# A hybrid trunk layer in fp32 on one core: the second head's query splits are placed behind the first head's maximum, head 0's rows get a queue of their own, and the interleaving table changes

## The chip, the cores and the metric

One core of a Trainium2 chip. The metric is device time in microseconds, from the start to the end of the program on that core. The kernel before was timed in 3 runs: median 1436.8 us, lowest 1436.42, highest 1437.74. A further execution was recorded by the hardware profiler; all profile numbers come from it.

The engines are TensorE (PE, with its weight loads as a row of their own, PEld), VectorE (DVE), ScalarE (ACT), GpSimd (POOL) and SyncE (SP). DMAs can be issued from SP, ACT and POOL. Each engine works through its instructions in order.

## The reference

One layer of a streaming encoder for two groups of rows that share the weights: 1024 frames of a new stream and 32 next frames of a running stream (so 1056 rows, width 1024). Three groups of heads read one input projection; their outputs are joined and go through an output projection; then comes an MLP with squared ReLU, with a layer norm after each half.

```python
proj = x @ prm['w_in']
q_lat, kv_lat, k_rope_raw, u, p_rwkv = jnp.split(proj, IN_SPLITS, axis=-1)
mla_out = mla_mixer(q_lat, kv_lat, k_rope_raw, ...)     # attention, 6 heads
s5_out = s5_mixer(u, ...)                               # S5 diagonal SSM, 16 groups
rwkv_out = rwkv_mixer(p_rwkv, ...)                      # RWKV-7 scan, 6 heads of 64
merged = jnp.concatenate([mla_out, s5_out, rwkv_out], -1)
x = layer_norm(ALPHA * x + merged @ prm['w_out'], ...)
x = layer_norm(ALPHA * x + jnp.square(jax.nn.relu(x @ prm['w_up'])) @ prm['w_down'], ...)
```

The attention's queries are what the change touches: `rms_norm(q_lat) @ w_qb` gives each head 64 columns without rotation ("nope") and 32 that are rotated ("rope"). The rotation is `x*cos + concat(-x2, x1)*sin` over the two halves of the 32. The new stream's queries see keys in chunks of 64 (chunk-causal); the running stream's queries see 512 cached keys and their own 32. Everything is float32.

## The kernel before

**Arithmetic.** A float32 matrix product is made of three reduced-precision ones: each operand x is split into hi (a copy by ACT, L49) and lo = x - hi (a subtraction by DVE, L50), and `mm3` issues hi*hi (L63), lo*hi (L65) and hi*lo (L67) into one PSUM tile. So every operand costs one ACT and one DVE instruction per piece before PE can use it.

**Stages.** Input projection; then `stage_q`, which makes the queries; then `middle`, where attention, the scan and S5 share the engines; then the output projection and the MLP, which take more than half of the time and in which PE is nearly always busy.

**`stage_q`** computes the queries of all six heads as products of 128 rows (two heads' nope columns; or the rope columns of heads 0 to 3 in one tile `qrope`, those of heads 4 and 5 in one of 96 rows, `qropeb`), rotates the rope tiles on DVE (`turn`), and writes the rows of each head into a DRAM buffer `q_d`: 64 nope rows and two pieces of 16 rope rows. In the kernel before, SP issues the writes of heads 0 and 1 (nope) and of the rope pieces of heads 0 to 3; POOL issues the others. In this stretch DVE also ends the inversion of the scan's triangular matrices; its result goes through DRAM (`zt_d` L782, `xt_d` L783) and comes back in another layout as `zb` and `zc` (L794, L795), from which PE builds further pieces with 32x32 products (L805).

**Attention in `middle`.** `attn_setup` issues on SP the loads of the rotated keys (`kr`), head 0's query rows (`q0`, 96 rows), the cached latents (`ct`) and cached rope keys (`kt`), and the extra rows 96 to 127 of the split queries. `attn_first` makes the keys of head 0 (`sck`, L1144), splits keys and queries, and computes, per block of 128 queries, the scores (L63/65/67 into `sc`) whose row maximum (`mx`, L1304) DVE takes. When all nine blocks are done, DVE joins the two halves (`m`, L1309), PE transposes the result (`scm`, L1311), ACT and DVE split it (`mh`, `ml`), and four small DMAs put it into row 96 of the split queries, so that the later score products have the maximum already subtracted. The cached latents and keys are transposed by PE (`sct`) and copied by ACT to `cpast` and `kpast` (L1118); the keys of the cached part need both. `attn_q` loads the next head's rows into the same buffer (tag "q", one buffer, so the load waits until the last head's split has read it) and splits them.

**Order.** Four generators yield after each small step: F (scores and maxima, head by head), O (probabilities, products with the values), S (scan), X (S5). A string of letters, `PLAN`, says whose step comes next; the order of PE's instructions is pinned by it (`issue_after` makes the scheduler place an instruction behind a given one). The other engines' instructions are placed by a list scheduler that respects data, buffers and these marks; the scan's steps have a higher priority. So changing a letter moves PE's work and, through the scheduler, the work of DVE, ACT and the queues.

Of the kernel before, what the change touches and what calls it, by code (L numbers as in the profile page):

```python
# [17 lines left out]
P = 128  # L18
T = 1056
# [26 lines left out]
def split3(g, ps, hi, lo, lo_eng=None):  # L46

    nc = g.nc
    nc.scalar.activation(out=hi, in_=ps, func=AF.Copy)  # L49
    (lo_eng or nc.vector).tensor_tensor(out=lo, in0=ps, in1=hi.bitcast(F32), op=ALU.subtract)  # L50
# [679 lines left out]
def hsl(i):  # L730
    return slice(64 * i, 64 * i + 64)
# [352 lines left out]
def attn_setup(g):  # L1084

    nc = g.nc
    g.wkv = g.ap0.tile([P, 2, 384], F32, tag="wkv", name="wkv")
    nc.sync.dma_start(out=g.wkv, in_=g.a["w_kvb"])
    g.kh, g.kl, g.q2 = [], [], []
    g.kr = g.ap.tile([P, 13 * 3 * 64], F32, tag="vo", name="kr", bufs=1)[:, :T]  # L1090
    nc.sync.dma_start(out=g.kr[64:128], in_=g.kr_d[0:64])
    g.q0 = g.ap.tile([P, T], F32, tag="q", name="q", bufs=1)
    nc.sync.dma_start(out=g.q0[0:96], in_=g.q_d[0])
    g.cpast = g.ap0.tile([P, 512], F32, tag="cpast", name="cpast")
    g.ct = g.ap.tile([P, 4, P], F32, tag="rec", name="ct", bufs=1)
# [38 lines left out]
def attn_first(g):  # L1134

    nc = g.nc
    attn_setup(g)
    qh, ql = g.qs[0] = g.q2[0]  # L1140

    def key(pool, tag, src):
        ps = pool.tile([P, 512], F32, tag=tag, name="sck")
        nc.tensor.matmul(out=ps[:, :src.shape[-1]], lhsT=g.wkv[:, 0, 0:P], rhs=src, start=True, stop=True)  # L1144
        return ps

    def smooth(ps, i, o, n):
        split3(g, ps[hsl(i), :n], g.kh[i][0:64, o:o + n], g.kl[i][0:64, o:o + n])

    def turned(x, c, o, n):  # L1150
        split3(g, x[64:128, c:c + n], g.kh[0][64:128, o:o + n], g.kl[0][64:128, o:o + n])

    def query(s, n):
        split3(g, g.q0[0:96, s:s + n], qh[0:96, s:s + n], ql[0:96, s:s + n])

    mx = attn_max(g, 0, qh, ql)
# [12 lines left out]
    query(512, 544)
    for _ in range(2):  # L1170
        next(mx)
        yield
    c = key(g.pav, "av", g.cpast)
    for _ in range(2):
        next(mx)
        yield
    d = key(g.psc, "sc", g.ckv[:, TP:T])
    turned(g.kpast, 0, TP, 512)
    turned(g.kr, TP, 1536, TS)
    for i in range(2):  # L1180
# [12 lines left out]

def attn_values(g, p):
# [16 lines left out]
def stage_q(g):  # L1211


    nc = g.nc
    i = 0

    def f(name):
        return g.p1.tile([P, T], F32, tag="f", name=name, bufs=5)

    def product(out, w):  # L1220
        nonlocal i
        for s, n in BLK:
            pool, tag = ((g.pfs, "fs"), (g.pt, "pt"))[i % 2]
            i += 1
            ps = pool.tile([P, 512], F32, tag=tag, name="scq")[:, :n]
            for k in range(2):
                nc.tensor.matmul(out=ps[:out.shape[0]], lhsT=w[:, k], rhs=g.qn[:, k, s:s + n], start=k == 0, stop=k == 1)
            nc.scalar.activation(out=out[:, s:s + n], in_=ps[:out.shape[0]], func=AF.Copy)

    wa = f("wqa")[:, :768].rearrange("p (k h c) -> p k h c", k=2, c=64)  # L1230
    wr = f("wqr")[:, :512].rearrange("p (k j x) -> p k j x", k=2, x=P)
    for k in range(2):
        nc.sync.dma_start(out=wa[:, k], in_=g.a["w_qb"][:, k, :, 0:64])
        for h, n, c, j, x in ((0, 4, 64, 0, 0), (0, 4, 80, 0, 64), (4, 2, 64, 1, 0), (4, 2, 64, 1, 32), (4, 2, 80, 1, 64)):
            nc.scalar.dma_start(out=wr[:, k, j, x:x + 16 * n].rearrange("p (h c) -> p h c", c=16), in_=g.a["w_qb"][:, k, h:h + n, c:c + 16])
    qs_ = g.xp.tile([P, KD, T], F32, tag="xl", name="qnope")

    def nope(p):
        q = qs_[:, KD - 3 + p]
        product(q, wa[:, :, 2 * p:2 * p + 2].rearrange("p k h c -> p k (h c)"))  # L1240
        for h in range(2):
            (nc.gpsimd if p else nc.sync).dma_start(out=g.q_d[2 * p + h, 0:64], in_=q[hsl(h)])

    cs, sn = f("ropec"), f("ropes")
    for h in range(4):
        nc.sync.dma_start(out=cs[32 * h:32 * h + 32], in_=g.a["rope"][0:32])
        for a in range(2):
            nc.sync.dma_start(out=sn[64 * a + 16 * h:64 * a + 16 * h + 16], in_=g.a["rope"][48 - 16 * a:64 - 16 * a])

    def turn(name, m, w, heads):  # L1250

        q, t = (g.p1.tile([P, 1152], F32, tag="kk", name=x, bufs=3)[:, :T] for x in (name, name + "t"))
        product(q[0:m], w)
        r = m - 64
        for a in range(2):
            nc.vector.tensor_tensor(out=t[64 * a:64 * a + r], in0=q[64 - 64 * a:64 - 64 * a + r], in1=sn[64 - 64 * a:64 - 64 * a + r], op=ALU.mult)
        nc.vector.tensor_tensor(out=q[0:m], in0=q[0:m], in1=cs[0:m], op=ALU.mult)
        for x in ((slice(0, P),) if r == 64 else (slice(0, r), slice(64, m))):
            nc.vector.tensor_tensor(out=q[x], in0=q[x], in1=t[x], op=ALU.add)
        yield  # L1260
        for j, h in enumerate(heads):
            for a in range(2):
                (nc.sync if h < 4 else nc.gpsimd).dma_start(out=g.q_d[h, 64 + 16 * a:80 + 16 * a], in_=q[64 * a + 16 * j:64 * a + 16 * j + 16])

    ta, tb = turn("qrope", P, wr[:, :, 0], range(4)), turn("qropeb", 96, wr[:, :, 1, 0:96], (4, 5))
    next(ta)
    nope(0)
    next(ta, None)
    next(tb)
    nope(1)  # L1270
    nope(2)
    next(tb, None)


def attn_q(g, h):

    nc = g.nc
    qh, ql = g.q2[h % 2]
    q = g.ap.tile([P, T], F32, tag="q", name="q", bufs=1)
    nc.sync.dma_start(out=q[0:96], in_=g.q_d[h])  # L1280
    if h > 1:
        for x in (qh, ql):
            nc.sync.dma_start(out=x[96:97].bitcast(F32), in_=g.kr_d[33:34])
    for s, n in ((0, 512), (512, 544)):
        split3(g, q[0:96, s:s + n], qh[0:96, s:s + n], ql[0:96, s:s + n])
        yield
    return qh, ql

# [110 lines left out]
def middle(g, scan):  # L1399
# [36 lines left out]


PLAN = (
    "FFFFFFFFSSSSSFFFFFFFFFFFFFFOFFOOSOSSOOOOFOSOSOSOSFSOFOFOOOOOOOOSSXOFSFSOXOFOFOOOOOOSFSFOSSOSXSOFXFSF"
    "OFOSOFXFSFOOSOSFSSOOXOSFSFOSFSOOFOXOOXOFFOSSOFSOOFXOFOOOSOOXOOOSFFOOXOOOSFOSSSFXSSFFOSFOSFFSSFXFFFSF"  # L1440
    "SFOXOFOSOSFXOOSFOOSOSSXOOFOSSOOXOSOFXOOOOOOOFSFOSSOFSSSOXOXOSOOOOFOOFFSFFOXFFFSSFFSSOOXSOSSFFSOXSFOS"
    "OOXOOSOOOFSOOOOOFSOFOOOOFSXOXOFXOXSOSOFXFOSSOOSOSFOSSFXOOOOSSFOXFSFFFSFFFSFFSFFFFSXFSFFOSSXOSOOFSOXO"
    "FOSFSOOOFXOSOOOFSOXFOSSXOSFOOOSOOOOOFXOOSSSSFOOOFFXSOXFOOSOSFSSOOFSFSFFOOSOOOOOOSOOOOSOOOOSOFOOSSOOO"
    "SOOSSOOSOOSOOOOOOOOO"
)


# [1032 lines left out]
```

## Time and profile before

| | |
|---|---|
| median of 3 runs | 1436.8 us (1436.42 to 1437.74) |
| profiled execution, whole | 1437.9 us |
| its span (first to last instruction) | 1436.1 us |
| mean granted PE clock | 0.972 of full |
| busy: PE / PEld / DVE / ACT / POOL | 96% / 86% / 69% / 45% / 8% |
| matrix products | 11520 |
| DMA | 199.48 MB in 149814 packets, mean 139 GB/s |

How to read the rows that follow: a timeline row gives start and length in us, engine, line of the kernel, operation, output and inputs by the program's names, shape, a count, and in brackets how long the engine had been idle before and what released it. A window row gives the busy time of each engine in a stretch, the clock that PE was granted, and the share of the 16 DMA engines in use. A PE that is busy at half clock counts as busy.

### The profile page before, as it was taken

The page shows a single profiled execution, that of the slowest core. Times are in us where ns is not written, and L with a number is a line of the kernel's source. Part 1 is how long each engine was busy: PE and PEld are TensorE (multiplying, and loading weights), DVE is VectorE, ACT ScalarE, POOL GpSimd, SP SyncE. Part 2 cuts the span into 40 slices and gives each one's busy share as a digit, 9 for nine tenths or more (in the row PEclk, how much of TensorE's full clock was granted, in tenths as well). Part 3 has the DMA queues.
Part 4 walks back from the last instruction along what each step waited for, and adds up shares of the span by engine and source line. Part 5 has one row for each costly group of instructions (what it writes and reads, how often), then busy time and mean ns, then how long its engine had stood idle before and what let it go on. Part 6 is the DMA issues. An engine that isn't in the chain of part 4 may idle for free.

```text
span 1436.1 us, 28225 instructions
## 1 busy us (share of the span) xinstructions
PE 1379.4 (96%) x11520; PEld 1241.1 (86%) x11520; DVE 984.5 (69%) x1793; ACT 641.8 (45%) x1129; POOL 112.4 (8%) x228
## 2 busy tenths in 40 slices
PE   9999999699999989999999999999999999999996
PEld 9989898576777767767788999999999999999996
DVE  7676969755566746565869966666655786665577
ACT  6646543324435554552336444443445443434332
POOL 1201300400000000110300000000000000000022
PEclk9999999789799999999999999999999999999998
DMA  5434554852332321244434543444339695354232
GB/s 205 149 125 143 172 158 98 207 124 55 92 101 75 86 80 35 75 133 137 121 107 150 182 154 142 142 143 162 132 118 390 222 322 166 96 176 135 64 103 77
DMA packets 149814, 199.48 MB, mean 139 GB/s; under 512 B 54424, under 2 KB 97100, under 8 KB 149176
## 3 DMA queue, kind: packets, MB, share of 16 engines
q1 hardware_dynamic: 128540, 177.72, 38.8%
q10 hardware_dynamic: 20424, 17.80, 4.1%
q0 software_dynamic: 720, 2.16, 0.5%
q8 instruction: 90, 1.47, 0.4%
q14 instruction: 40, 0.33, 0.1%
HBM read 130.03 MB, written 67.55 MB: 138 GB/s over the span
## 4 chain that ended last, share of the span: by engine, by line
PE 82%; DVE 8%; DMA 4%; ACT 2%; issue 2%; SPq 1%; ACTq 0%; DVEq 0%; POOL 0%; POOLq 0%
PE acc L63 20%; PE acc L67 20%; PE acc L65 20%; PE av L1333 3%; PE sc L63 1%; DMA wo<-in_w_out 1%; PE st L63 1%; PE st L65 1%; PE st L67 1%; PE prt L857 1%; DVE mx L1304 1%; PE sc L67 1%; PE sc L65 1%; PE pti L805 1%; DMA q<-q_d 1%
## 5 line engine op out<-in xcount | busy, mean ns | idle before, releaser
L67 PE MATMUL acc<-xo,wo 128*128 128x256 f32 (+1 forms) x896 | 253.7, 284 | 2.8 <-DVE wo L50 2.6
L63 PE MATMUL acc<-xo,wo 128*128 128x272 f32 (+1 forms) x896 | 254.1, 284 | 0.1
L65 PE MATMUL acc<-xo,wo 128*128 128x272 f32 (+1 forms) x896 | 253.3, 283 | 0.1
L67 PE MATMUL acc<-hop,wo 128*128 128x272 f32 (+1 forms) x896 | 194.4, 284 | 0.0
L67 PEld LDWEIGHTS acc<-xo,wo 128*128 128x128 f32 x896 | 167.9, 188 | 3.6 <-DVE wo L50 3.6
L65 PEld LDWEIGHTS acc<-xo,wo 128*128 128x128 f32 x896 | 168.5, 188 | 0.4 <-DVE xo L50 0.3
L63 PEld LDWEIGHTS acc<-xo,wo 128*128 128x128 f32 x896 | 168.2, 188 | 0.3 <-ACT wo L49 0.3
L63 PE MATMUL acc<-hop,wo 128*128 128x256 f32 (+1 forms) x768 | 159.1, 285 | 0.0
L65 PE MATMUL acc<-hop,wo 128*128 128x272 f32 (+1 forms) x768 | 158.3, 283 | 0.0
L67 PEld LDWEIGHTS acc<-hop,wo 128*128 128x128 f32 x896 | 142.4, 188 | 0.0
L63 PE MATMUL acc<-xh,wmhi 128*128 128x384 f32 (+3 forms) x384 | 126.9, 331 | 2.0 <-ACT ckv L207 1.7
L65 PE MATMUL acc<-xl,wmhi 128*128 128x384 f32 (+3 forms) x384 | 127.5, 332 | 0.7 <-DVE xl L50 0.6
L67 PE MATMUL acc<-xh,wmlo 128*128 128x384 f32 (+3 forms) x384 | 126.1, 329 | 0.0
L65 PEld LDWEIGHTS acc<-hop,wo 128*128 128x128 f32 x768 | 119.6, 189 | 0.0
L63 PEld LDWEIGHTS acc<-hop,wo 128*128 128x128 f32 x768 | 118.7, 188 | 0.0
L49 ACT ACTIVATE wo<-wr 128x512 fp32r<-128x512 f32 (+1 forms) x64 | 46.9, 738 | 119.6 <-PE acc L67 69.8
L50 DVE TENSOR_TENSOR hop<-hraw,hop 128x1056 fp32r<-128x1056 f32 (+3 forms) x58 | 70.4, 1214 | 14.9 <-ACT hop L49 14.9
L50 DVE TENSOR_TENSOR wo<-wr,wo 128x512 fp32r<-128x512 f32 (+1 forms) x64 | 52.4, 821 | 40.1 <-ACT wo L49 40.0
L1333 PE MATMUL av<-ptk,vo 128*128 128x512 f32 (+5 forms) x204 | 77.2, 463 | 1.2 <-ACT po L1338 0.5
L63 PEld LDWEIGHTS acc<-xh,wmhi 128*128 128x128 f32 (+1 forms) x384 | 71.2, 185 | 5.1 <-ACT ckv L207 1.8
L65 PEld LDWEIGHTS acc<-xl,wmhi 128*128 128x128 f32 (+1 forms) x384 | 71.1, 185 | 4.5 <-DVE xl L50 1.3
L49 ACT ACTIVATE hop<-hraw 128x1056 fp32r<-128x1056 f32 (+3 forms) x58 | 60.6, 1046 | 30.7 <-PE acc L67 28.8
(554 smaller groups left out, 2987.7 us busy)
## 6 DMA issues: line engine op xcount, KB each, us to landing
hraw<-h_d SPq DMA_DIRECT2D x48, 528.0 KB
wr<-in_w_up SPq DMA_DIRECT2D x35, 512.0 KB
h_d<-hx SPq DMA_DIRECT2D x16, 792.0 KB
h_d<-ht SPq DMA_DIRECT2D x16, 792.0 KB
wd<-in_w_dn SPq DMA_DIRECT2D x16, 512.0 KB
wr<-in_w_dn SPq DMA_DIRECT2D x16, 512.0 KB
ld<-rw SPq DMA_DIRECT2D x24, 320.0 KB
wmraw<-in_w_m SPq DMA_DIRECT2D x12, 512.0 KB
```

The costliest lines, as they stand in the source:

```text
L49: nc.scalar.activation(out=hi, in_=ps, func=AF.Copy)
L50: (lo_eng or nc.vector).tensor_tensor(out=lo, in0=ps, in1=hi.bitcast(F32), op=ALU.subtract)
L63: nc.tensor.matmul(out=outs[i], lhsT=lh, rhs=rhs[i][0], start=start, stop=False, **kw)
L65: nc.tensor.matmul(out=outs[i], lhsT=lh, rhs=rhs[i][1], start=False, stop=False, **kw)
L67: nc.tensor.matmul(out=outs[i], lhsT=ll, rhs=rhs[i][0], start=False, stop=stop, **kw)
L805: nc.tensor.matmul(out=ps[64 * c:64 * c + 32, t], lhsT=l[rows, t], rhs=z[rows, t], start=True, stop=True)
L857: nc.tensor.transpose(out=pt[:, i], in_=ld[:, p, i], identity=g.ident)
L1304: nc.vector.tensor_reduce(out=mx[:n, t, b // 512:b // 512 + 1], in_=ps[:n, :w], axis=AX.X, op=ALU.max)
L1333: nc.tensor.matmul(out=po[:, c:n], lhsT=vo[:w, kt].rearrange("p a x -> p (a x)")[:, 64 * i:64 * i + P], rhs=pt[:w, c:n], start=kt == tiles ...
```

## The change

Five edits:

1. Head 0's query load goes to the end of `attn_setup`, so on SP it is issued after the loads of `kr`, `ct`, `kt` and the extra rows.
2. `attn_first` notes its last ACT instruction (the copy `mh` of head 0's maximum) as `g.front`, and head 1's two splits are issued after it.
3. SP issues the three writes of head 0's rows; POOL issues all the others.
4. The rope columns of heads 4 and 5 are laid out over 128 rows, like those of heads 0 to 3 (two more weight loads on ACT's queue, products of 128 rows in place of 96), so that the rotation ends in one addition over 128 rows in place of two over 32.
5. `PLAN` is a new string; its first two lines are shown below.

```diff
@@ attn_setup
     nc.sync.dma_start(out=g.kr[64:128], in_=g.kr_d[0:64])
-    g.q0 = g.ap.tile([P, T], F32, tag="q", name="q", bufs=1)
-    nc.sync.dma_start(out=g.q0[0:96], in_=g.q_d[0])
     g.cpast = g.ap0.tile([P, 512], F32, tag="cpast", name="cpast")
...
     nc.gpsimd.dma_start(out=g.kpast[96:128], in_=g.kr_d[32:64, 0:512])
+    g.q0 = g.ap.tile([P, T], F32, tag="q", name="q", bufs=1)
+    nc.sync.dma_start(out=g.q0[0:96], in_=g.q_d[0])
@@ attn_first
     yield from mx
+    g.front = last_traced(g, mybir.EngineType.Activation)
@@ stage_q
-        for h, n, c, j, x in ((0, 4, 64, 0, 0), (0, 4, 80, 0, 64), (4, 2, 64, 1, 0), (4, 2, 64, 1, 32), (4, 2, 80, 1, 64)):
+        for h, n, c, j, x in ((0, 4, 64, 0, 0), (0, 4, 80, 0, 64), (4, 2, 64, 1, 0), (4, 2, 64, 1, 32), (4, 2, 80, 1, 64), (4, 2, 80, 1, 96)):
...
-            (nc.gpsimd if p else nc.sync).dma_start(out=g.q_d[2 * p + h, 0:64], in_=q[hsl(h)])
+            (nc.gpsimd if p + h else nc.sync).dma_start(out=g.q_d[2 * p + h, 0:64], in_=q[hsl(h)])
...
-    def turn(name, m, w, heads):
+    def turn(name, w, heads):
...
-        for x in ((slice(0, P),) if r == 64 else (slice(0, r), slice(64, m))):
-            nc.vector.tensor_tensor(out=q[x], in0=q[x], in1=t[x], op=ALU.add)
+        nc.vector.tensor_tensor(out=q, in0=q, in1=t, op=ALU.add)
         yield
         for j, h in enumerate(heads):
             for a in range(2):
-                (nc.sync if h < 4 else nc.gpsimd).dma_start(out=g.q_d[h, 64 + 16 * a:80 + 16 * a], in_=q[64 * a + 16 * j:64 * a + 16 * j + 16])
-
-    ta, tb = turn("qrope", P, wr[:, :, 0], range(4)), turn("qropeb", 96, wr[:, :, 1, 0:96], (4, 5))
+                (nc.gpsimd if h else nc.sync).dma_start(out=g.q_d[h, 64 + 16 * a:80 + 16 * a], in_=q[64 * a + 16 * j:64 * a + 16 * j + 16])
+
+    ta, tb = turn("qrope", wr[:, :, 0], range(4)), turn("qropeb", wr[:, :, 1], (4, 5))
@@ attn_q
-        split3(g, q[0:96, s:s + n], qh[0:96, s:s + n], ql[0:96, s:s + n])
+        with g.tc.issue_after(g.front) if h == 1 else nullcontext():
+            split3(g, q[0:96, s:s + n], qh[0:96, s:s + n], ql[0:96, s:s + n])
@@ middle's table
-    "FFFFFFFFSSSSSFFFFFFFFFFFFFFOFFOOSOSSOOOOFOSOSOSOSFSOFOFOOOOOOOOSSXOFSFSOXOFOFOOOOOOSFSFOSSOSXSOFXFSF"
-    "OFOSOFXFSFOOSOSFSSOOXOSFSFOSFSOOFOXOOXOFFOSSOFSOOFXOFOOOSOOXOOOSFFOOXOOOSFOSSSFXSSFFOSFOSFFSSFXFFFSF"
+    "FFFFFFFSSFSFSSFFFFFFFFFFFFFOFFOOSOSOSOOFOOSOSOSOSFSOFOFOOOOOOOOSSXOFSFSOXOFOFOOOOOOSFSFOSSOSXFSOFXSF"
+    "OFOSOFXFSFOOSOSFSSXOOOSFSFOFSSOOFFOOOOXSSXOFSOOFOOOFOFXSOOOOSOOFOXOFOOXOOSFSSSFXSSFFOSFOSFFSSFXFFFSF"
...
```

What the scheduler makes of it, at three places. First ACT, from the end of head 0's query split on (`qh<-q` is a query split, 96x512 the first piece of a head and 96x544 the second; `cpast` and `kpast` are the cached latents and keys; `mh` is the copy of the transposed maximum). Before:

```order
L49 ACTIVATE qh<-q 96x544
L1118 ACTIVATE cpast<-sct 128x512
L49 ACTIVATE qh<-q 96x512
L49 ACTIVATE qh<-q 96x544
L1118 ACTIVATE kpast<-sct 32x512
L49 ACTIVATE kh<-kpast 64x512
L49 ACTIVATE kh<-sck 64x512
L49 ACTIVATE kh<-sck 64x32
L49 ACTIVATE kh<-sck 64x512
L49 ACTIVATE kh<-sck 64x32
L49 ACTIVATE mh<-scm 9x128
```

and with the change:

```order
L49 ACTIVATE qh<-q 96x544
L1118 ACTIVATE cpast<-sct 128x512
L1118 ACTIVATE kpast<-sct 32x512
L49 ACTIVATE kh<-kpast 64x512
L49 ACTIVATE kh<-sck 64x512
L49 ACTIVATE kh<-sck 64x32
L49 ACTIVATE kh<-sck 64x512
L49 ACTIVATE kh<-sck 64x32
L49 ACTIVATE mh<-scm 9x128
L49 ACTIVATE qh<-q 96x512
L49 ACTIVATE qh<-q 96x544
```

The two splits of head 1 moved from between `cpast` and `kpast` to behind `mh`.

Second, PE at the same place, after head 0's sixth score block of the first pass (`sck` are the keys' products, `pti` the scan's 32x32 products, and the number behind `n_` tells their operands apart). Before:

```order
L1144 MATMUL sck<-cpast,wkv 128x512
L1144 MATMUL sck<-ckv,wkv 128x32
L805 MATMUL pti<-zb,n_1372 32x32 x32
L805 MATMUL pti<-zb,n_1278 32x32 x32
L805 MATMUL pti<-zc,n_1182 32x32 x32
L805 MATMUL pti<-zb 32x32 x32
L63 MATMUL sc<-kh,qh 128x512
```

and with the change:

```order
L805 MATMUL pti<-zb,n_1372 32x32 x32
L1144 MATMUL sck<-cpast,wkv 128x512
L1144 MATMUL sck<-ckv,wkv 128x32
L805 MATMUL pti<-zb,n_1278 32x32 x32
L63 MATMUL sc<-kh,qh 128x512
L65 MATMUL sc<-kl,qh 128x512
L67 MATMUL sc<-kh,ql 128x512
L805 MATMUL pti<-zc,n_1182 32x32 x32
L805 MATMUL pti<-zb 32x32 x32
```

One group of 32x32 products moved ahead of the two key products, and one block of scores moved into the middle of the others.

Third, DVE at the end of head 1's maxima (`ces` are S5's state rows, `gq` and `r` the scan's; `m` is the joined maximum). Before:

```order
L660 SCALAR_TENSOR_TENSOR ces<-ces 128x536
L934 TENSOR_TENSOR gq<-pru,pc 128x192
L870 TENSOR_TENSOR r<-ld 128x3x128
L664 TENSOR_TENSOR ces<-ces 128x1072
L871 TENSOR_TENSOR r<-r,vec 128x3x128
L1304 TENSOR_REDUCE mx<-sc 32x1
L665 TENSOR_TENSOR ces<-ces 128x536
L1309 TENSOR_TENSOR m_3848<-mx 128x9
```

and with the change:

```order
L660 SCALAR_TENSOR_TENSOR ces<-ces 128x536
L1304 TENSOR_REDUCE mx<-sc 32x1
L1309 TENSOR_TENSOR m_3849<-mx 128x9
L934 TENSOR_TENSOR gq<-pru,pc 128x192
L870 TENSOR_TENSOR r<-ld 128x3x128
L664 TENSOR_TENSOR ces<-ces 128x1072
L871 TENSOR_TENSOR r<-r,vec 128x3x128
L665 TENSOR_TENSOR ces<-ces 128x536
```

The last maximum and the joining step moved ahead of five instructions of the scan and of S5.

On SP, the loads of `zb` from `zt_d` (L794) now stand ahead of head 1's query load, and those from `xt_d` (L795) behind it; before, that load stood ahead of both. On PE, S5's product `s5e` (L646) stands behind two more pairs of attention products than before.

More of the change, by code (lines that the diff above doesn't have):

```diff
@@ L1226, in product @@
             for k in range(2):
-                nc.tensor.matmul(out=ps[:out.shape[0]], lhsT=w[:, k], rhs=g.qn[:, k, s:s + n], start=k == 0, stop=k == 1)
-            nc.scalar.activation(out=out[:, s:s + n], in_=ps[:out.shape[0]], func=AF.Copy)
+                nc.tensor.matmul(out=ps, lhsT=w[:, k], rhs=g.qn[:, k, s:s + n], start=k == 0, stop=k == 1)
+            nc.scalar.activation(out=out[:, s:s + n], in_=ps, func=AF.Copy)
     wa = f("wqa")[:, :768].rearrange("p (k h c) -> p k h c", k=2, c=64)
@@ L1248, in stage_q @@
             nc.sync.dma_start(out=sn[64 * a + 16 * h:64 * a + 16 * h + 16], in_=g.a["rope"][48 - 16 * a:64 - 16 * a])
-    def turn(name, m, w, heads):
+    def turn(name, w, heads):
         q, t = (g.p1.tile([P, 1152], F32, tag="kk", name=x, bufs=3)[:, :T] for x in (name, name + "t"))
-        product(q[0:m], w)
-        r = m - 64
+        product(q, w)
         for a in range(2):
-            nc.vector.tensor_tensor(out=t[64 * a:64 * a + r], in0=q[64 - 64 * a:64 - 64 * a + r], in1=sn[64 - 64 * a:64 - 64 * a + r], op=ALU.mult)
-        nc.vector.tensor_tensor(out=q[0:m], in0=q[0:m], in1=cs[0:m], op=ALU.mult)
-        for x in ((slice(0, P),) if r == 64 else (slice(0, r), slice(64, m))):
-            nc.vector.tensor_tensor(out=q[x], in0=q[x], in1=t[x], op=ALU.add)
+            nc.vector.tensor_tensor(out=t[64 * a:64 * a + 64], in0=q[64 - 64 * a:P - 64 * a], in1=sn[64 - 64 * a:P - 64 * a], op=ALU.mult)
+        nc.vector.tensor_tensor(out=q, in0=q, in1=cs, op=ALU.mult)
+        nc.vector.tensor_tensor(out=q, in0=q, in1=t, op=ALU.add)
         yield
@@ L1438 @@
 PLAN = (
-    "FFFFFFFFSSSSSFFFFFFFFFFFFFFOFFOOSOSSOOOOFOSOSOSOSFSOFOFOOOOOOOOSSXOFSFSOXOFOFOOOOOOSFSFOSSOSXSOFXFSF"
-    "OFOSOFXFSFOOSOSFSSOOXOSFSFOSFSOOFOXOOXOFFOSSOFSOOFXOFOOOSOOXOOOSFFOOXOOOSFOSSSFXSSFFOSFOSFFSSFXFFFSF"
[L1441 to L1444, printed above, removed]
+    "FFFFFFFSSFSFSSFFFFFFFFFFFFFOFFOOSOSOSOOFOOSOSOSOSFSOFOFOOOOOOOOSSXOFSFSOXOFOFOOOOOOSFSFOSSOSXFSOFXSF"
+    "OFOSOFXFSFOOSOSFSSXOOOSFSFOFSSOOFFOOOOXSSXOFSOOFOOOFOFXSOOOOSOOFOXOFOOXOOSFSSSFXSSFFOSFOSFFSSFXFFFSF"
+    "SFOXOFOSOSFXOOSFOOSOSSXOSOFOSOOXOSOFXOOFOOOOOFSFOSSOSSSOXOXOSOOOOFOOFFSFFOXFFFSSFFOSSOXSOSSFFSOXSFOS"
+    "OOXOOSOOOFSOOOOOFOSOFOOOFOSXOXFXOSXSFOOFXSSOOSOSOFSSOFXOOOOSSFOXFSFFFSFFSFFSFFFFSFXFSFFOSSXOSOOFSOXO"
+    "FOOSFSOOFOXSOOOFSOOXFSOSXOOOSFSOOOOOFXOOSSSSFOOOFFXSOXFOOSOSFSSOOFSFSFFOOSOOOOOOOSOOOSOOOOSOFOOSSOOO"
+    "SOOSSOSOOOOSOOOOOOOO"
 )
```

## The prediction

> **What bounds the kernel now.** First the page: busy shares and the 40 slices of 35.9 us.
>
> ```profile
> PE 1379.4 (96%) x11520; PEld 1241.1 (86%) x11520; DVE 984.5 (69%) x1793; ACT 641.8 (45%) x1129; POOL 112.4 (8%) x228
> PE   9999999699999989999999999999999999999996
> PEclk9999999789799999999999999999999999999998
> ```
>
> TensorE (PE) sets the time: 96% busy at a clock near full. The exceptions are slices 8 (251 to 287 us, busy 6, clock 7) and 9 (clock 8) and a dip in slice 11 (clock 7). A late start there is paid in full, because PE has no idle time later in which to make it up. So I looked at slices 8 to 11, first by windows (columns: length; busy us and instructions of PE, weight load, DVE, ACT, POOL; granted clock; DMA share; GB/s).
>
> ```profile
> 267.11:270.52 3.41, 3.41 (x14) 2.81 (x13) 1.32 (x5) 0.60 (x1) 3.41 (x4) 0.50 0.95 292
> 270.52:273.93 3.41, 1.36 (x9) 1.06 (x7) 0.69 (x1) 0.00 (x0) 0.17 (x1) 1.00 0.99 238
> 273.93:277.35 3.42, 0.00 (x0) 0.00 (x0) 0.61 (x1) 1.25 (x3) 0.00 (x0) 0.50 0.64 84
> 280.76:287.59 6.83, 6.50 (x244) 6.40 (x238) 5.96 (x11) 0.68 (x2) 4.84 (x6) 0.50 0.90 195
> 294.41:297.83 3.42, 2.54 (x16) 1.38 (x15) 2.48 (x7) 0.27 (x1) 0.11 (x1) 1.00 0.05 7
> 277.90:294.40 16.50, 16.01 (x276) 13.23 (x277) 12.82 (x24) 1.97 (x5) 6.94 (x7) 0.50 0.90 198
> 271.90:297.06 25.16, 17.80 (x285) 13.84 (x285) 16.31 (x30) 3.74 (x8) 6.94 (x7) 0.59 0.79 162
> ```
>
> The granted clock changes in steps of 3.41 us. It was 0.50 after a step with 1.36 us busy, came back after one with 3.41, did not come back through 6.50 of 6.83 made up mostly of 32x32 products, and stayed at 1.00 through 2.54. So the empty place around 274 costs twice: 6 us of no work, then 16.5 us of work at half clock. The timeline gives its cause, with one line of the chain of waits (the second: start, length, what).
>
> ```profile
> 271.61 0.27 PE L67 MATMUL sc<-kh,ql 128*128 128x128 f32 x1
> 266.59 9.46 DMA q<-q_d
> 276.08 1.18 ACT L49 ACTIVATE qh<-q 96x512 fp32r<-96x512 f32 x2 [7.39 <-DMA q<-q_d]
> 276.74 1.32 DVE L50 TENSOR_TENSOR ql<-q,qh 96x512 fp32r<-96x512 f32 x2 [5.52 <-ACT qh L49]
> 277.28 0.58 ACT L1118 ACTIVATE kpast<-sct 32x512 f32<-32x512 f32 x1
> 277.92 2.07 PE L1144 MATMUL sck<-cpast,wkv 128*128 128x512 f32 x2 [6.03 <-ACT kpast L1118]
> 297.06 0.28 PE L1311 MATMUL scm<-ident,m 128*9 128x128 f32 x1 [0.67 <-DVE m L1309]
> 297.37 0.27 ACT L49 ACTIVATE mh<-scm 9x128 fp32r<-9x128 f32 x1 [14.93 <-PE scm L1311]
> 297.41 0.28 PE L67 MATMUL sc<-kh,ql 128*128 128x128 f32 x1
> ```
>
> Head 1's rows take 9.46 us to land, ACT runs in order, so kpast sits behind the split of rows that nobody needs before 297, and PE stands from 271.88 to 277.92.
>
> **The change part by part**, against the profiled execution's 1437.9 us (span 1436.1); the median, 1436.8, lies 1.1 below it.
>
> *A, the front (rotation over 128 rows, queues, late load).*
>
> ```profile
> 254.75 2.51 DVE L1256 TENSOR_TENSOR qropebt<-qropeb,ropes 32x1056 f32<-32x1056 f32 x2
> 258.58 2.53 DVE L1259 TENSOR_TENSOR qropeb<-qropeb,qropebt 32x1056 f32<-32x1056 f32 x2
> 259.91 0.59 ACT L49 ACTIVATE kh<-sck 64x512 fp32r<-64x512 f32 x1 [0.45 <-PE sck L1144]
> 261.14 2.64 DVE L50 TENSOR_TENSOR kl<-sck,kh 64x512 fp32r<-64x512 f32 x4
> 264.36 1.18 ACT L49 ACTIVATE qh<-q 96x512 fp32r<-96x512 f32 x2
> 264.10 0.18 POOL L1295 MEMSET mx<- 128x18 f32 x2
> 266.79 0.29 DVE L1304 TENSOR_REDUCE mx<-sc 128x1 f32<-128x128 f32 x1
> 252.53 3.56 SPq L1263 DMA_DIRECT2D q_d<-qrope  x8
> 260.12 0.99 POOL L1263 DMA_DIRECT2D q_d<-qropeb  x2 [2.77 <-DVE qropeb L1259]
> ```
>
> Two additions of 1.26 become one; kl can then start at 261.14 - 1.26 = 259.88, but waits for kh until 259.91 + 0.59 = 260.50: a gain of 0.64, bounds 0 and 1.26. Take -0.6. Six qrope writes of 0.45 leave SP, and head 0's load moves behind four others there; it still goes out near 257, some 7 us ahead of its split at 264.36, which covers it. On POOL the six add 6 x 0.5 = 3.0 us, which fits into its idle time before 260. The cover there is the 2.5 us between the mx memset and its first use at 266.79; without it, up to +3. Take 0.
>
> *B, the empty place.* The split moves behind mh, kpast is copied near 271, and nothing of head 1 stands before the keys. What is late next is the scan's tables: the new order puts PE's first product with zb (L805) ahead of sck<-cpast. Below: SP's loads of zb, its waits (total, times, longest), the transfer ahead of them, and a window.
>
> ```profile
> 266.95 5.24 SPq L794 DMA_DIRECT2D zb<-zt_d  x4
> SPq L1280 <- DVE sc L1303: 4.7, 1, 4.7
> SPq L795 <- DMA xt_d<-y: 1.5, 1, 1.5
> xt_d<-y SPq DMA_DIRECT2D x1, 864.0 KB
> 258.75:273.00 14.25, 8.54 (x32) 6.12 (x30) 10.04 (x19) 5.82 (x11) 9.59 (x15) 0.76 1.02 310
> ```
>
> SP no longer holds those loads behind head 1's load (which waited 4.7 us, until 266.59), but the transfers are at a share of 1.02, so they land when the bytes ahead are through. The first two of four were issued by about 269.6; head 1's own load took 9.46, of which 1.3 are its own 96 x 1056 x 4 bytes at 310 GB/s. I estimate that PE gets its first zb at 274: bounds 271.9 (no hole) and 277.9 (nothing won). A hole of 2 us leaves some 1.4 us busy in a step, as in the 270.52 row, so the clock falls all the same and the 16.0 us of work run mostly at half: 274 + 16.0 = 290.0, plus the 2.66 from 294.40 to scm = 292.7 against 297.06. A clock that recovers a step earlier adds about 0.6. Take -5. The far bound is DVE: 16.31 busy less head 1's 1.32 = 15.0, so scm at 286.9, -10.2; the near bound 0.
>
> *C, a new wait.* After scm, head 1's first score with ql came 0.35 later. Now it waits for scm 0.28, mh 0.27, one qh 0.59, one ql 0.66 and hops, about 1.9: +1.5. Queued behind it are the values' products (scv), and behind mh on ACT their copies. If that idle time drops a clock step, dense products bring it back after one step, +1.7; at about two in five I add 0.7. Take +2.2, bounds 1.0 and 3.5.
>
> *D, head 1's maximum.* On DVE it stands now ahead of L934, L870, L664, L871, L665.
>
> ```profile
> 348.18 0.28 PE L1311 MATMUL scm<-ident,m 128*9 128x128 f32 x1 [2.92 <-DVE m L1309]
> 345.61:349.03 3.42, 0.85 (x9) 0.52 (x11) 3.38 (x7) 1.54 (x5) 1.00 (x5) 1.00 0.02 5
> 349.03:352.44 3.41, 3.41 (x28) 2.27 (x25) 1.44 (x5) 1.38 (x3) 0.16 (x1) 0.50 0.04 7
> ```
>
> The stall of 2.92 goes and with it the half-clock step (3.41 / 2 = 1.7): -4.6 at most. What moves behind the maximum is then late for the scan, up to the whole stall. Take -3, bounds -4.6 and 0.
>
> *E, S5's products.* s5e goes behind two more pairs of attention products.
>
> ```profile
> 372.72 1.04 PE L646 MATMUL s5e<-ut,em 128*128 128x133 f32 x4 [1.69 <-DVE yc L1011]
> 369.51:372.92 3.41, 1.72 (x22) 1.58 (x20) 3.10 (x14) 2.28 (x6) 0.11 (x1) 1.00 0.53 125
> 372.92:393.40 20.48, 18.71 (x157) 14.57 (x156) 8.89 (x20) 7.44 (x20) 0.30 (x2) 0.50 0.43 117
> 383.22 1.27 DVE L656 TENSOR_TENSOR ces<-ces 128x1072 f32<-128x1072 f32 x1 [2.99 <-DMA gate<-rw]
> ```
>
> If the 1.69 is filled, the half-clock stretch behind it might go too, up to 18.71 / 2 = 9.4; but DVE is busy 3.10 of 3.42 there, and a later s5e makes L656 later. Take -1, bounds +3 and -6.
>
> *F.* The other moves are of single products; bounded by the largest stall quoted behind 300, 2.92, both ways. Take 0.
>
> Sum: -0.6 - 5 + 2.2 - 3 - 1 = -7.4, so 1430.5 for a profiled execution and **1429.4** for the median. D and E pass on in full, since PE is the bound behind them.
>
> **The rivals.** (1) *The clock stays up at 274* and DVE sets scm at 286.9: B -10.2, C +1.5, the sum -13.3, 1423.5. For it: 2.54 busy kept 1.00. Against: 1.36 and 1.72 did not. The Trainium skill (TensorE: Matmul & The Clock Gate, "HAM oscillation") has it so: "no PE-idle gaps >~3.4µs", by which a hole of 2 us costs no clock and the sum would be this rival's; the 1.69 gap ahead of 372.72 was followed by a clock of 0.50, so the trace does not agree here. (2) *The change moves the hole rather than closing it*: zb lands near 277.4, because xt_d's 864 KB are ahead of it (SP waited 1.5 for them), and L805 now bars sck. B -0.5, the sum -2.9, 1433.9. For it: the share of 1.02; against: 1.3 us of bytes less ahead. (3) *Slower*: the wait C leaves a step with 1.72 us busy or less (the 369.51 row), and what follows are scv and again 32x32 products, which did not bring it back at 280.76; then a stretch like that of 372.92 begins at scm. Its price is 9.4, and 2.5 for the work at full clock of the 294.41 row; in place of C's 0.7 that makes the sum +3.8, 1440.6. For it: C adds 1.5 idle to a step that had 2.54 busy. Against: the first work behind the wait is scv's, 128 rows deep and dense.
>
> **How the numbers follow.** Forecast 0.50, with its own range 1425 to 1433 (D between its bounds, or B 3 off either way); rival 1 0.20, rival 2 0.20, rival 3 0.10. The range 1420 to 1436 leaves out rival 3 and the tails. A measurement of this kernel can tell 0.2% (2.9 us) from no change, so faster is below 1433.9: 0.46 of the forecast, all of rival 1, half of rival 2, 0.76; same 0.15; slower 0.09.
>
> **What would show it.** Right: no idle time before sck released by kpast; PE's wait before L805 released by zb, 2 us long; kl some 0.6 earlier; a wait of about 1.5 us at the score with ql behind scm; no stall at head 1's scm. The forecast is wrong if scm of head 0 stands later than 296 or earlier than 289, if a half-clock stretch follows it, or if s5e's new place moves L656 later by more than 2 us.

## The result, and the profile after

The changed kernel takes 1425.2 us (median of 4 runs, 1421.4 to 1427.1) against 1437.3: 0.9913 of the time before, 95% interval 0.9891 to 0.9936. Timed again beside other kernels it was 0.9916 (0.9896 to 0.9937). The forecast was 1429.4 with the range 1420 to 1436; the gain is 12 us where the sum gave 7.4. The profiled execution took 1421.4, the fastest of the four; that of x7, the same program profiled again, took 1429.5, the slowest of its six. All times and ratios here are of runs in the fast state; one of the 12 runs of x6, with 3348.6 us, was in the slow one and is left out.

The page of the changed kernel (span, busy shares, the clock in 40 slices):

```profile
span 1419.5 us, 28231 instructions
PE 1368.5 (96%) x11520; PEld 1233.9 (87%) x11520; DVE 983.4 (69%) x1792; ACT 641.1 (45%) x1129; POOL 115.9 (8%) x235
PEclk9999999899999999999999999999999999999998
```

The same 11520 products keep PE busy for 10.9 us less (1379.4 to 1368.5), at a mean granted clock of 0.982 in place of 0.972, and PE is idle for 51.0 us in place of 56.7. So two thirds of what these two executions differ by is work that no longer runs at half clock, and one third is idle time that is gone. In x7's execution the two parts are 4.0 and 4.4 us, about half each.

The places that the prediction spoke of, in the timeline of the changed kernel:

```profile
261.76 0.47 PE L63 MATMUL sc<-kh,qh 128*128 128x128 f32 x1 [3.96 <-ACT qh L49]
...
267.53 0.59 ACT L1118 ACTIVATE kpast<-sct 32x512 f32<-32x512 f32 x1 [2.12 <-PE sct L1117]
269.38 1.40 PE L805 MATMUL pti<-zb,n 32*32 32x32 f32 x64 [0.84 <-DMA zb<-zt_d]
270.70 1.13 PE L1144 MATMUL sck<-cpast,wkv 128*128 128x512 f32 x2
...
275.17 0.22 PE L805 MATMUL pti<-zc,n 32*32 32x32 f32 x2 [1.18 <-DMA zc<-zt_d]
...
286.10 0.28 PE L1311 MATMUL scm<-ident,m 128*9 128x128 f32 x1 [0.56 <-DVE m L1309]
286.71 1.18 ACT L49 ACTIVATE qh<-q 96x512 fp32r<-96x512 f32 x2
288.11 0.47 PE L67 MATMUL sc<-kh,ql 128*128 128x128 f32 x1
288.38 2.02 PE L1206 MATMUL scv<-wkv,ckv 128*128 128x128 f32 x8
...
337.93 0.27 PE L1311 MATMUL scm<-ident,m 128*9 128x128 f32 x1
```

kpast no longer waits for head 1's rows. PE's hole ahead of the keys is 0.84 us and ends with zb's landing; a second wait, 1.18 for zc, stands at 275.17. From the first score to head 0's scm it is 24.34 us, before it was 31.92 (265.14 to 297.06). Behind scm the new wait stands: the values' products (scv) come 2.28 later, before it was 0.46, with scm at 297.06:

```profile
297.52 1.11 PE L1205 MATMUL scv<-wkv,ckv 128*128 128x128 f32 x8
```

Head 1's scm has no wait in front of it.

The windows of the changed kernel, cut where its clock steps:

```profile
266.97:270.38 3.41, 2.57 (x63) 2.03 (x62) 2.93 (x5) 1.21 (x2) 2.52 (x6) 1.00 0.68 143
270.38:273.79 3.41, 3.41 (x95) 2.54 (x88) 3.27 (x7) 1.03 (x3) 3.41 (x4) 1.00 1.27 182
273.79:277.21 3.42, 1.89 (x99) 1.61 (x100) 2.85 (x6) 0.32 (x2) 1.40 (x1) 1.00 0.56 99
277.21:284.03 6.82, 6.82 (x56) 5.16 (x50) 5.09 (x10) 0.00 (x0) 0.00 (x0) 0.50 1.07 221
284.03:287.45 3.42, 1.44 (x9) 0.52 (x7) 2.02 (x7) 1.01 (x3) 0.11 (x1) 1.00 1.07 243
287.45:290.86 3.41, 3.39 (x15) 3.20 (x16) 1.65 (x4) 0.85 (x2) 0.00 (x0) 0.50 0.06 10
...
372.78:379.61 6.83, 5.75 (x32) 3.89 (x33) 4.07 (x12) 3.35 (x8) 0.12 (x1) 0.50 0.02 4
```

The half-clock stretches around 280 and 376 are 6.82 and 6.83 long; before both were 20.48. The step lost to the new wait is 287.45 to 290.86. And there is a new hole: PE does nothing from 368.3 to 373.0. Its cause, in the timeline:

```profile
365.11 1.07 SPq L641 DMA_DIRECT2D ces<-tab_d  x1
370.44 1.28 DVE L656 TENSOR_TENSOR ces<-ces 128x1072 f32<-128x1072 f32 x1 [5.58 <-DMA mg_d<-ot]
372.96 0.69 PE L63 MATMUL sc<-kh,qh 128*128 128x384 f32 x1 [4.66 <-DVE mx L1304]
```

PE's score waits for a maximum that stands on DVE behind L656, and L656 waits 5.58 for a transfer. The profile names mg_d<-ot, the last transfer that landed; run x8 below shows which it was.

**Chance ahead of the change.** PE's instructions ahead of the query products (scq) are the same in all these kernels, but their times are not. The first scq in the kernel before, in the changed one and in x7, the changed one profiled again:

```profile
241.10 1.46 PE L1227 MATMUL scq<-qn,wqr 128*128 128x384 f32 x4
```

```profile
238.17 1.46 PE L1228 MATMUL scq<-qn,wqr 128*128 128x384 f32 x4
```

```profile
242.66 1.46 PE L1228 MATMUL scq<-qn,wqr 128*128 128x384 f32 x4
```

4.5 us lie between two executions of one program. The changed kernel's first profiled execution came 2.93 early to that product. From it to the end of the span it takes 1181.3 us, before 1195.0: 13.7 less; x7 takes 1185.0, 10.0 less. So below, stages are compared by lengths from a product to a product inside one execution, and times by the ratios of many runs.

How far some executions are ahead of the kernel before, each counted from its own first scq, at the products (scm) that end the maxima of heads 0, 1 and 2, and at the end (us; the kernel before gets there after 55.96, 107.08, 184.77 and 1195.0):

| execution | head 0 | head 1 | head 2 | end |
|---|---|---|---|---|
| the change, first profile | 8.0 | 7.3 | 11.7 | 13.7 |
| the change again (x7) | 5.8 | 6.1 | 9.2 | 10.0 |
| edits 1 to 4, old table (x3) | 6.5 | 1.9 | 1.9 | 1.9 |
| the table alone (x2) | 2.4 | 5.9 | 11.5 | 11.7 |
| three letters (x5) | 1.4 | 4.4 | 10.3 | 5.0 |

Each row is one execution. x5, x6 and x10 change nothing ahead of head 0's maximum and are 0.4 to 1.4 ahead there, so about that much is chance.

### The profile page after: what moved, and what is told of

The parts are those of the page before. It is cut to its first block, busy times and chain, and to the rows that moved or that the text cites. A ratio compares the mean times of both kernels' runs of the same rounds, so it can differ in the third digit from the quotient of the medians.

```text
span 1419.5 us, 28231 instructions
## 1 busy us (share of the span) xinstructions
PE 1368.5 (96%) x11520; PEld 1233.9 (87%) x11520; DVE 983.4 (69%) x1792; ACT 641.1 (45%) x1129; POOL 115.9 (8%) x235
## 4 chain that ended last, share of the span: by engine, by line
PE 82%; DVE 8%; DMA 4%; issue 2%; SPq 2%; ACT 2%; ACTq 0%; DVEq 0%; POOL 0%; POOLq 0%
PE acc L63 20%; PE acc L67 20%; PE acc L65 20%; PE av L1333 3%; PE scq L1228 1%; PE sc L63 1%; DMA wo<-in_w_out 1%; PE st L65 1%; PE sc L67 1%; PE st L63 1%; PE st L67 1%; PE sc L65 1%; PE prt L857 1%; PE scv L1206 1%; DVE mx L1304 1%
```

## The experiments

All ratios are to the kernel before, timed on the same chip in the same rounds.

**x1: the hold alone.**

```diff
 attn_first:      yield from mx
+    g.front = last_traced(g, mybir.EngineType.Activation)
 attn_q:
+        with g.tc.issue_after(g.front) if h == 1 else nullcontext():
```

> The kernel before with edit 2 alone (head 1's splits issued behind head 0's maximum); table, queues, rotation and loads as before. Theory H (the gain in the stretch 272 to 297 comes from the hold): kpast is copied near 271 and the hole shrinks; scm of head 0 moves about 5 us forward (zb is still loaded behind head 1's query load, so not the whole 7.6), the new wait behind scm costs 2 to 3: about 1434, 2 to 4 below before. Rival T (the table makes the gain, the hold alone none): PE gets its first 32x32 products only when zb lands, the hole moves, and the new wait is paid: 1437 to 1439.

Measured: 0.9991 (0.9979 to 1.0003), no change that can be told. Its timeline:

```profile
264.79 0.47 PE L63 MATMUL sc<-kh,qh 128*128 128x128 f32 x1 [4.30 <-ACT qh L49]
...
275.76 3.00 PE L805 MATMUL pti<-zb,n 32*32 32x32 f32 x128 [3.14 <-DMA zb<-zt_d]
293.61 0.28 PE L1313 MATMUL scm<-ident,m 128*9 128x128 f32 x1 [0.81 <-DVE m L1311]
295.78 1.11 PE L1206 MATMUL scv<-wkv,ckv 128*128 128x128 f32 x8
```

The stretch to scm is shorter (28.82), but the hole has moved: PE now waits 3.14 for zb, as in the second rival of the prediction; SP still issues head 1's load ahead of zb here. And 1.7 us are paid back behind scm (2.17 in place of 0.46). The time lies between what theory H and rival T expected.

**x2: the table alone** (the five lines of `PLAN`, nothing else).

> The kernel before with edit 5 alone (the new table). Theory H: the hole at 272 to 278 stays, since head 1's split still stands ahead of kpast on ACT; the table brings only what lies behind 300: head 1's maximum (-4.2 in the trace of the change), S5's products (-2.6) and the rest (-2.0), so about 1428.5 to 1430. Rival T: the 32x32 products ahead of the keys fill the hole and nearly all of the gain is here: 1425 to 1426.

Measured: 0.9927 (0.9912 to 0.9942), 10.5 us: nearly all of the change's gain. By the time rival T is right, but not by its mechanism. In the timeline:

```profile
262.86 0.48 PE L63 MATMUL sc<-kh,qh 128*128 128x128 f32 x1 [4.30 <-ACT qh L49]
...
274.47 2.04 PE L805 MATMUL pti<-zb,n 32*32 32x32 f32 x64 [4.83 <-DMA zb<-zt_d]
292.51 0.28 PE L1311 MATMUL scm<-ident,m 128*9 128x128 f32 x1 [0.55 <-DVE m L1309]
292.97 1.11 PE L1205 MATMUL scv<-wkv,ckv 128*128 128x128 f32 x8
340.07 0.27 PE L1311 MATMUL scm<-ident,m 128*9 128x128 f32 x1
```

The hole is still 4.83 and the stretch to scm 29.65. Most of the gain lies behind: there is no wait ahead of head 1's scm, and of the 11.7 us that this execution is ahead at the end, 2.4 are there at head 0's scm and 11.5 at head 2's.

**x3: the change with the old table** (edits 1 to 4).

> The changed kernel with the old table (edits 1 to 4). Theory H: the stretch up to head 0's scm is won (A -0.4, B -7.6 in the trace), the wait behind it paid (+3.0), nothing behind 345: about 1432. Rival T: within 1 of before, 1436 to 1438. If 1 to 4 give more than x1 by over 2 us, the queues and the rotation matter, too.

Measured: 0.9984 (0.9973 to 0.9995). Edits 1 to 4 together bring 0.7 to 3.9 us, less than theory H had said. In its trace the stretch to scm is 25.85 (265.01 to 290.86), 3 shorter than x1's. zb is loaded ahead of head 1's rows, and PE meets it without a wait; a hole stands at zc instead:

```profile
278.32 0.28 PE L805 MATMUL pti<-zc,n 32*32 32x32 f32 x2 [3.25 <-DMA zc<-zt_d]
```

This execution is 6.5 us ahead at head 0's scm, but only 1.9 at head 1's. In between stand the new wait behind scm and two half-clock steps (293.88 and 321.18) that the kernel before does not have. By the time of the whole, x1 and x3 can't be told apart.

**x4: the hold one step earlier**, so that the splits stand ahead of `mh`.

```diff
         smooth(x, 1, o, 512)
+    g.front = last_traced(g, mybir.EngineType.Activation)
     yield from mx
-    g.front = last_traced(g, mybir.EngineType.Activation)
```

> The changed kernel with head 1's splits held only behind the splits of the keys, so that they stand ahead of the maximum's copy (mh) on ACT. Theory H: the new wait behind scm (1.66 of wait, 1.3 more of half clock) goes, B stays: about 2.5 below the change, 1422.7. Rival: DVE is the bound up to scm, so the two lo splits of 1.32 only move ahead of scm and the clock's step is lost anyway: within 1 of the change, 1424 to 1426.

Measured: 0.9900 (0.9881 to 0.9920), median 1422.6. The wait behind scm is gone:

```profile
293.57 0.28 PE L1311 MATMUL scm<-ident,m 128*9 128x128 f32 x1 [0.56 <-DVE m L1309]
294.03 1.11 PE L1206 MATMUL scv<-wkv,ckv 128*128 128x128 f32 x8
```

0.46 as before, where the change has 2.28. The median is 3.8 below x7's, but the intervals overlap: that the wait goes is shown, that the whole gains is not.

**x5: three letters of the table** (94 to 96), which move head 1's last scores.

```diff
-    ...SOSXSOFXFSF"
+    ...SOSXFSOXFSF"
```

> The kernel before with three letters of the table changed (letters 94 to 96, SOF to FSO), which move head 1's last 32x32 scores, and with them the joined maximum on DVE, ahead of a block of the scan; nothing else. If step D is right by itself: the 2.92 stall at head 1's scm and the half-clock step behind it go, -3 to -4.5, so 1433 to 1434.5. Rival (the stall only moves to the scan's instructions that fall behind, and the table gains only as a whole): 1436.5 to 1438.

Measured: 0.9952 (0.9934 to 0.9970), about 6.9 us, twice what the step was said to be worth. In its timeline and windows:

```profile
347.40 0.27 PE L1311 MATMUL scm<-ident,m 128*9 128x128 f32 x1
```

```profile
367.08:370.49 3.41, 1.63 (x23) 1.46 (x20) 3.06 (x13) 1.65 (x5) 0.11 (x1) 1.00 0.52 123
370.49:384.14 13.65, 13.42 (x127) 12.34 (x127) 6.49 (x15) 5.55 (x15) 0.21 (x1) 0.50 0.65 176
```

The 2.92 stall is gone with the half-clock step behind it. Beyond that, the next half-clock stretch is 13.65 in place of 20.48, two steps fewer, with S5's products where they were. That shows one way in which a gain grows on its way: this execution is 10.3 us ahead at head 2's scm. But later it pays half of that back: at head 4's scm (548.51, before 550.35) it is 5.4 ahead. In between lie a wait of 4.93 at 508, where the kernel before has 3.67, and two more half-clock steps. The profiled execution is the slowest of the nine (1436.5); whether the others pay less back, one profile can't say.

**x6: S5's products alone** (letters 119 to 175).

> The kernel before with letters 119 to 175 of the new table alone (S5's products: s5y earlier, s5e behind two more pairs, and the attention steps around them). If the gain between 360 and 400 seen in the change (-2.1) and in the table alone (-3.7) is this step's: 1433.5 to 1435.5. Rival (in the change PE then waits 4.66 at 368 for a maximum that stands on DVE behind L656, so this step gives nothing and the gain there came from elsewhere): 1437 to 1439.

Measured: 1.0001 (0.9985 to 1.0018). Alone, the move is worth nothing: its trace has the hole at the score's maximum, 4.49 long, as the change has (4.66), and a shorter half-clock stretch in exchange.

**x7: the change once more.**

> The changed kernel once more, to compare with x4 and x8 on one chip and to see how much of its profiled -2.9 ahead of 240 us, where its code is that of before, is chance. If it is chance: median 1425 to 1426, and the products at 240 lie between -3 and +2 of before. If the edits caused it: -2.9 again.

Measured: 0.9916 (0.9896 to 0.9937), 1426.4. Its first scq stands at 242.66, 1.56 later than before, where the first profile was 2.93 early, so that was chance. And the stretch to scm, in the same program:

```profile
266.26 0.48 PE L63 MATMUL sc<-kh,qh 128*128 128x128 f32 x1 [3.97 <-ACT qh L49]
274.79 2.08 PE L805 MATMUL pti<-zb,n 32*32 32x32 f32 x64 [1.73 <-DMA zb<-zt_d]
292.80 0.28 PE L1311 MATMUL scm<-ident,m 128*9 128x128 f32 x1 [0.56 <-DVE m L1309]
```

```profile
271.67:275.08 3.41, 1.68 (x16) 1.24 (x15) 2.96 (x5) 1.21 (x2) 2.34 (x6) 1.00 0.55 107
275.08:288.73 13.65, 13.65 (x269) 10.93 (x270) 9.68 (x18) 1.35 (x4) 4.81 (x4) 0.50 0.96 173
...
292.14:295.56 3.42, 1.54 (x12) 1.14 (x11) 2.29 (x7) 1.44 (x3) 0.11 (x1) 1.00 0.22 34
295.56:298.97 3.41, 3.41 (x17) 3.41 (x16) 1.50 (x5) 0.60 (x1) 0.00 (x0) 0.50 0.31 71
```

26.54 in place of 24.34. The hole is a little longer and lies wholly in one clock step, which ends with 1.68 us busy; then 13.65 us run at half clock rather than 6.82. Behind scm, the step with the new wait has 1.54 us busy, and again a half-clock step follows.

**x8: S5's table loaded first**, on top of x4.

```diff
+        nc.sync.dma_start(out=tb[:, 0:2], in_=g.tab_d[:, :, gs])
         for s in range(8):
             nc.sync.dma_start(out=tz[s:P:L5, :, 16 * s:P], in_=g.kt_d[:, gs, 0:(8 - s) * 16])
...
-        nc.sync.dma_start(out=tb[:, 0:2], in_=g.tab_d[:, :, gs])
```

> x4 (early hold) with one more edit: S5's table (the load of tab_d into ces) is issued ahead of the eight loads of kt_d rather than behind them. Theory: the 4.66 for which PE waits at 368 in the change is DVE waiting in L656 for that table, which SP issues only behind those eight and what is mixed with them; issued 7 us earlier the hole goes, and the half-clock steps behind it (about 6 us of work at half clock): 5 to 8 below x4, 1415 to 1418. Rival (L656 waits for S5's products or their copies, not for the table): within 1.5 of x4, 1421 to 1424.

Measured: 0.9869 (0.9849 to 0.9889), median 1419.6: the fastest kernel here, 18.7 below before in the median, and its interval lies below the change's. In its timeline:

```profile
357.25 0.61 SPq L639 DMA_DIRECT2D ces<-tab_d  x1
364.20 1.28 DVE L656 TENSOR_TENSOR ces<-ces 128x1072 f32<-128x1072 f32 x1 [0.49 <-DMA ld<-rw]
```

In x4, to which this edit was added, the same instruction waits as in the change:

```profile
374.70 1.28 DVE L656 TENSOR_TENSOR ces<-ces 128x1072 f32<-128x1072 f32 x1 [6.03 <-DMA mg_d<-ot]
```

The table goes out 7.9 us earlier than in the change (7.7 counted from the first scq), L656 waits 0.49, and no score waits for a maximum near 370. In x11, which has the same edit, L656 does not wait either. So the transfer that L656 waited for was the table, not `mg_d<-ot`, which the profile named. The median is 3.0 below x4's, less than the 5 to 8 that were expected, and the two intervals overlap: that the hole goes is shown, what it is worth in the whole is not settled.

**x9: the first 96 letters** of the new table, with edits 1 to 4.

> The changed kernel with the new table's first 96 letters only (the scan's tables ahead of the keys, head 1's maximum moved), the old letters behind. If the parts add up from x3 (-2.1) and x5 (-7.6): 1428 to 1429.5. If the rest of the table (S5's products and the later letters) is needed for the change's -11.8: that leaves 2 to 3 for it. Rival (head 1's maximum gains less once the stretch ahead of it is short): 1431 to 1433.

Measured: 0.9977 (0.9962 to 0.9992), 1434.0: less than x5 alone, as the rival said, but for a reason that neither named. In its timeline, near the keys and near 505:

```profile
274.77 2.12 PE L805 MATMUL pti<-zb,n 32*32 32x32 f32 x64 [4.75 <-DMA zb<-zt_d]
...
505.22 1.28 ACT L700 ACT_TABLE_LOAD   x1 [3.86 <-DMA mg_d<-ot]
506.52 1.98 ACT L700 ACTIVATE zt<-zt 128x2128 f32<-128x2128 f32 x1
508.51 1.28 ACT L76 ACT_TABLE_LOAD   x1
509.81 0.67 ACT L1358 ACTIVATE ptk<-st 32x32 f32<-32x32 f32 x2
510.05 0.63 PE L1333 MATMUL av<-ptk,vo 32*128 32x32 f32 x2 [8.79 <-ACT ptk L1358]
```

The scheduler has put an attention step (`ptk`) on ACT behind S5's gelu (L700), which waits 3.86 for a transfer and swaps ACT's function table before and behind itself: PE stands for 8.79. In the kernel before and in the change, PE's wait at that place is shorter: 3.67 at 513.43 and 3.01 at 497.75. So x9 carries a hole of some 5 us there that the change does not have.

It also has a hole of 4.75 ahead of zb, and a stretch to scm of 29.79 (263.19 to 292.98), although its queues are those of the change. So it does not measure its letters cleanly.

**x10: the late letters alone** (from 176).

> The kernel before with the new table's letters from 176 on alone (head 2's maximum and later). If the -2.0 seen behind 400 in the change's trace is theirs: 1435.5 to 1436.5. Rival (it is the chance place of half-clock steps): within 0.7 of before.

Measured: 1.0010 (0.9995 to 1.0025). The same hole at S5's gelu is here (7.83, released by the same ACT step), so again a sum of two things; the late letters alone win nothing.

**x11: x8 with S5's products where they were** (letters 119 to 175 old).

> x8 with letters 119 to 175 as before (S5's products and the attention steps around them where they were). If the S5 moves gain once the table's load is early: 1421 to 1423. If they are worth nothing, as x6 says: 1418.5 to 1420.5.

Measured: 0.9892 (0.9870 to 0.9913), 1422.5, against x8's 0.9869 (0.9849 to 0.9889). It lies in the range of the first theory, that the S5 moves gain once the table is early, but the intervals overlap: inconclusive.

**x12: the early hold alone**, all else as before.

> The kernel before with the hold of x4 alone (head 1's splits behind the splits of the keys, ahead of mh), everything else as before. Against x1 (-1.9) it lacks the wait behind scm (1.7, and at times half a clock step): -3.5 to -5, 1433 to 1434.5. Rival (the two lo splits on DVE ahead of the last maxima cost as much): -1 to -2, 1436.

Measured: 0.9991 (0.9978 to 1.0004), as x1, and as the rival said. Without the new queues the hold wins nothing that can be told, early or late.

## Why the prediction was right, and where its sizes were off

The direction held, and most steps were seen at their places; the sizes were not as forecast. A, B and C together were priced at -3.4, and edits 1 to 4 alone measure -2.3 (0.7 to 3.9 less, x3): that half of the sum is right in total, but not part by part: in x3's trace 6.1 us are won in B's stretch and 4.6 lost again between the scm of head 0 and that of head 1, where C had 2.2. D, E and F were priced at -4, and the table alone measures -10.5 (8.3 to 12.6 less, x2). The two measured halves add up to 12.8, the change has 12.0. So the terms that were too small are those of the table; that 12.0 still lies in the range is owed to its width (0.8 to 16.8 less than before), not to the sum.

Of the signs of being right, all came: no idle time before sck, a wait before L805 released by zb (0.84 and 1.73, where 2 was said), kl 0.6 earlier (19.43 us behind the first scq, before 20.04), a wait at the score with ql, no stall at head 1's scm. Of the three signs of being wrong, two came in the first profile: head 0's scm stands at 286.10, earlier than 289, of which 2.93 is the early start (x7: 292.80); and a half-clock step follows it, in both profiles. The third did not: L656 starts 132.3 us behind the first scq, before 142.1.

- **A, forecast -0.6.** From the first scq to the first score 23.59 (x7: 23.60), before 24.04: -0.45. Right, and steady: all seven profiles with edit 4 have 23.59 or 23.60, all others 23.93 or more. PE waits 3.96 for the query's split in place of 4.41 for a DMA.
- **B, forecast -5.** From 31.92 in the profile before to 24.34 and 26.54 in the two of the change: -7.6 and -5.4. The forecast had a PE start at 274, a hole of 2 and a clock that falls: x7 shows just that (a hole of 1.73, 13.65 us at half clock); the first profile had a shorter hole and a clock that fell later. With the hold and the old queues and rotation the stretch is 28.82 (x1) and 28.35 (x12); with edits 1, 3 and 4 added it is 25.85 (x3), and with the new table as well 24.34 to 27.88 in five profiles and 29.79 in one (x9). So the stretch is shorter with these edits in most executions, not in each, and which of them does it was not tried. Rival 1, the clock that stays up, came in part: in the first profile the clock stayed up through the hole at zb (2.57 us busy in its step) and the two steps behind it, and came down at 277.21, after a step with 1.89 us busy that holds the wait for zc, which the prediction did not name. Rival 2, the hole that moves, was seen too: to zb in x1, x2, x9 and x12 (3.14 to 4.83), to zc in x3 (3.25).
- **C, forecast +2.2.** 2.28 in place of 0.46: +1.8, and a half-clock step behind it in both profiles of the change (287.45 in the one above). Right in mechanism, and with the step's price (3.39 / 2 = 1.7) about 3.5, the upper bound. In x1 no half-clock step follows the same wait. x4 shows that the wait was avoidable.
- **D, forecast -3: the step whose size was most wrong.** The prediction took a discount because "what moves behind the maximum is then late for the scan". Of that nothing is seen next to the maximum: head 1's scm has no wait in x2, x5, x7 and the change, and up to 357 x5 has one PE wait of over half a us (0.65 for `ml`), where the kernel before has one of 0.62. From head 0's scm to head 1's x5 gains 3.0. But the prediction let the term end with its stall and the step behind it (-4.6 at most), and x5 gains 6.9 (4.3 to 9.5) by this move alone: PE comes sooner to S5's products, and the half-clock stretch there, which the prediction had under E, is shorter without E's move. Nor does it pass on in full, as the prediction said: that execution has lost half of its lead again by head 4's maximum.
- **E, forecast -1.** Nothing alone (x6). In the change it swaps a 20.48 us half-clock stretch for a hole of 4.66 and a stretch of 6.83. The danger was named (L656 late for its transfer), its place was not: the hole is PE waiting for a maximum behind L656. x8 takes it away.
- **F, forecast 0.** Late letters alone give nothing (x10). The table's parts that were run alone (x5, x6, x10) add up to about -5.3 of its -10.5. In part that is the hole at S5's gelu, which x10 has and the table as a whole has not. The letters ahead of 94 were not run alone, and E's move without the hole that it makes was measured only by x8 against x11, which is inconclusive. How much belongs to which letters stays open.

Rival 3, the half-clock stretch behind the new wait, came as one step and no more: the dense products behind the wait brought the clock back. In both profiles of the change a step with 1.4 to 1.9 us busy was followed by half clock. The Trainium skill's clock rule, which the prediction set beside rival 1 (TensorE: Matmul & The Clock Gate, "HAM oscillation"), asks for an idle gap of over about 3.4 us. By that rule none of these steps would have cost the clock, so here, too, the trace disagrees.

In x7 and in the first profile, one program ran 13.65 and 6.82 us at half clock in the same place. The same page of the Trainium skill ("What's actually happening") calls the window free-running, so that when the clock changes depends on where the work falls in it. The two profiles fit that, but they do not show it by themselves, because their holes at zb differ too (1.73 and 0.84).

## What to carry to other kernels

A stall on a PE-bound path is priced twice: its length, and the work behind it that runs at half clock; of the difference here half (x7) to two thirds (the first profile) is of the second kind. When a wait for the wrong data is taken away, ask which transfer the next instruction needs and whether its queue lets it out early: the hold alone moved the hole, and with the loads reordered it shrank in most executions. Ask, too, whether the time won at one place reaches the next: of x3's 6.5 us at head 0's maximum 1.9 were left at head 1's, because a new wait and half-clock steps stood in between. Do not judge an order table by its parts: the scheduler moves other engines' work with each letter, and a part can carry a stall that the whole does not have.

## What the runs showed of the hardware that was not expected

- **PE's busy time alone does not say what the clock will do.** In the windows shown so far, a step with 0.85 to 1.89 us of PE busy was followed by half clock, and one with 2.54 or more was not. Over whole traces that is no rule. In the change's own trace a step with 2.41 was followed by half clock:

```profile
311.34:314.75 3.41, 2.41 (x37) 2.03 (x33) 1.03 (x2) 1.03 (x3) 0.00 (x0) 1.00 0.89 272
314.75:318.16 3.41, 3.41 (x14) 3.01 (x14) 1.04 (x4) 2.12 (x7) 0.00 (x0) 0.50 0.14 33
```

In the same trace a step with 1.82 (167.98 to 171.39) kept the full clock, and in x7 a step that was busy throughout (87.34 to 90.76) lost it; 9 of its 17 products have 32 or 64 rows (32*128 and 64*128 in the timeline), the others 128. What else counts, these runs do not show.

- **32x32 products count as busy in the profile, but the clock did not come back while they ran:** in x7 the stretch from 275.08 is busy for 13.65 of 13.65 us and stays at half for four steps; 32x32 products run in it until 285.9, with larger ones between them. In the change, where they end at 278.2, 6.82 us were enough. No run tried them by themselves.
- **Chance on a fixed program.** The same product lay 4.5 us apart in two executions of one program, and with it the place where the holes fall in the clock's steps. The change's own runs lie 5.8 us apart; that this is why is argued, not tried.
